# Letting SSD groups two to four wait one product more between asking for the decays' rows and using them

## The chip, the cores and the metric

The kernel runs on one core of a Trainium2 chip. The core has five engines, each with its own queue, which it works off in order: TensorE (PE, matmuls and transposes), VectorE (DVE), ScalarE (ACT), GpSimd (POOL) and SyncE (SP). Data come from HBM by DMA. The metric is the device time of one execution in microseconds; the kernel before took 1976.08 us in the median of three runs (1975.45, 1976.08 and 1978.53).

## The reference

The kernel computes one layer of a decoder trunk for a sequence of 1024 positions of width 1024 in float32. Three token mixers share one input projection; the third is a Mamba-2 SSD, and it is the one that the change touches:

```
h  = h + W_out( sum_k sigmoid(g_k(xn)) * P_k(mixer_k(xn)) ),  xn = RMSNorm(h)
h  = h + W2 relu(W1 RMSNorm(h))^2
...
def ssd_mixer(z, xbc, dt_raw, conv_w, conv_b, dt_bias, a_log, d_skip, norm_g):
    xbc = jax.nn.silu(causal_dwconv(xbc, conv_w, conv_b))
    ...
    a_cs = jnp.cumsum(adt, axis=-1)
    decay = jnp.exp(segsum(adt))
    cb = jnp.einsum('bclgn,bcsgn->bgcls', cc, bc)
    y_diag = jnp.einsum('bgcls,bgrcls,bcsgrp->bclgrp', cb, decay, xdt)
    states = jnp.einsum('bcsgn,bgrcs,bcsgrp->cbgrpn', bc, decay_states, xdt)
    ...
    y_off = jnp.einsum('bclgn,cbgrpn,bgrcl->bclgrp', cc, prev, jnp.exp(a_cs))
    y = y_diag + y_off + x32 * d_skip
```

There are four SSD groups of four heads each, eight chunks of 128 positions, and beside them eight heads of a linear recurrence (RG-LRU) and eight groups of a gated MLP.

## The kernel before, in words

The stretch that matters here is the projection by single columns of 128, run by `run` and `one_unit`. A unit is a product of 128 output channels with all 1024 positions: 48 matmuls of 512 columns (L555), since each operand is split into a high and a low part and three of the four part products are taken. Behind the matmuls `one_unit` calls the unit's `post`, which evicts the product (a convolution for SSD and LRU channels: L576 on ACT, then three L578 on DVE; for a gate L235 to L238), and then `step`, which advances every pending generator to its next `yield`. So a `yield` in a generator is worth one product: what stands behind it is written behind the next product's matmuls. A weight tile of a unit is loaded two units ahead by SP, copied on ACT (L526 for the high part, L527 for the negative of it) and completed by an accumulating DMA on POOL (L528).

The units come in this order for each of the four SSD groups: the channels of B, C, x0 and x1 of the group, then two LRU heads (in the fourth group each head has a gate product behind it), and after all groups the eight gated-MLP products. The first of the two products behind a group's four is called A, the second B.

With x1's eviction a group enters `ssd_stages`. The positions are worked in two halves. `rows_in` asks for the decays' rows of a half: four DMAs on POOL (L657) broadcast rows of `acs_d` to all partitions, into two tiles `E` (named a in the profile). `s1_` asks for the rows' exponentials (L663, POOL), transposes x and B on PE (L669, L676) and multiplies C with B (L681); DVE evicts with L672, L673 and L684, ACT with L677; ACT turns the rows into decays with 16 L690 of 128 columns and two L691; DVE multiplies with L694. `s2_` makes the states (L703 on PE, L714 on DVE), `s3_` the outputs (L723 and L727 on PE, L729 to L731 on DVE) and stores them (L732, POOL). The `aux` tiles in PSUM that PE writes in all these steps come from a pool of four. The LRU heads have stages of their own (L789 on PE, L792 to L801 on ACT, L798 to L804 on DVE, a store L810 on POOL) that use the same pool.

Nothing fixes the order of a queue by hand: the framework orders each engine's instructions from the order in which the program writes them and its own estimate of when each can run. So an instruction may stand earlier in its engine's queue than the program text has it, if its inputs are expected early.

Of the kernel before, what the change touches and what calls it, by code (L numbers as in the profile page):

```python
# [36 lines left out]
def trunk_kernel(ctx: ExitStack, tc: tile.TileContext, x, norm_mix_g, w_in, b_gate, gmlp_ln_g, gmlp_ln_b,  # L37
# [37 lines left out]
    def half_(shape=(P, HF), dt=F32):  # L75
        return halfp.tile(list(shape), dt, tag="half", name=nm("h"))

    def aux():
        return auxp.tile([P, HF], F32, tag="aux", name=nm("aux"))
# [371 lines left out]
    for q in range(2):  # L451
# [3 lines left out]
        for i in range(4):  # L455
            g = q * 4 + i
# [167 lines left out]
    def ssd_units(g):  # L624
        S = {}

        def xbc(key, ct):
            def post(ps):
                c = act()
                conv(c, ps, [scw[:, j * 16 + ct:j * 16 + ct + 1] for j in range(4)], vh[:, SCB + ct:SCB + ct + 1])  # L630
                t = act()
                actv(t, c, AF.Tanh)
                stt(out=c, in0=t, scalar=1.0, in1=c, op0=ALU.add, op1=ALU.mult)
                S[key] = c
                if key == "x1":
                    later(ssd_stages(g, S))
            unit_in(C_XBC + ct * P, post)

        xbc("b", 8 + g)
        xbc("c", 12 + g)  # L640
        xbc("x0", 2 * g)
        xbc("x1", 2 * g + 1)

    def ssd_stages(g, S):
# [5 lines left out]
        def tok(c):  # L650
            return slice(c * P, (c + 1) * P)

        def rows_in(half):
            for q in (2 * half, 2 * half + 1):
                e = E[q] = act((P, 2, 4, P))
                for cc in range(2):
                    nc.gpsimd.dma_start(out=e[:, cc], in_=acs_v[0, 2 * q + cc, hs, :].partition_broadcast(P))  # L657

        def s1_(half):
            for j in range(2):  # L660
                t = er[half, j] = half_((P, 4, P))
                for h in range(2):
                    nc.gpsimd.dma_start(out=t[64 * h:64 * h + 64], in_=acs_v[1, half * 4:half * 4 + 4, 4 * g + 2 * j + h, :].partition_broadcast(64))  # L663
            for q in (2 * half, 2 * half + 1):
                ps = aux()
                for cc in range(2):
                    for j in range(2):
                        o = cc * 256 + j * P
                        nc.tensor.transpose(out=ps[:, o:o + P], in_=Xf[j][:, tok(2 * q + cc)], identity=ident)  # L669
                ev = ps.rearrange("p (c h d) -> p c h d", c=2, h=4)  # L670
                xdt[q], xw[q] = half_((P, 2, 4, 64)), half_((P, 2, 4, 64))
                tt(out=xdt[q], in0=ev, in1=dt[:, 2 * q:2 * q + 2, hs].unsqueeze(3).to_broadcast([P, 2, 4, 64]), op=ALU.mult)  # L672
                tt(out=xw[q], in0=ev, in1=w2[:, 2 * q:2 * q + 2, hs].unsqueeze(3).to_broadcast([P, 2, 4, 64]), op=ALU.mult)  # L673
            ps = aux()
            for i in range(4):
                nc.tensor.transpose(out=ps[:, tok(i)], in_=Bf[:, tok(half * 4 + i)], identity=ident)  # L676
            actv(Bt[:, half * 4:half * 4 + 4, :], ps.rearrange("p (c n) -> p c n", c=4), AF.Copy)  # L677
            cb[half] = aux()
            for i in range(4):
                c = half * 4 + i  # L680
                mm(cb[half][:, tok(i)], Bf[:, tok(c)], Cf[:, tok(c)], start=True, stop=True)  # L681

            cbm = half_((P, 4, P))
            tt(out=cbm, in0=cb[half].rearrange("p (c l) -> p c l", c=4), in1=tri.unsqueeze(1).to_broadcast([P, 4, P]), op=ALU.mult)  # L684
            for q in (2 * half, 2 * half + 1):
                e = E[q]
                for cc in range(2):
                    for h in range(4):
                        col = (2 * q + cc) * 16 + 4 * g + h
                        actv(e[:, cc, h, :], e[:, cc, h, :], AF.Relu, scale=-1.0, bias=acs[:, col:col + 1])  # L690
                actv(e, e, AF.Exp, scale=-1.0)  # L691
                for cc in range(2):
                    i = (2 * q + cc) % 4
                    tt(out=e[:, cc], in0=e[:, cc], in1=cbm[:, i].unsqueeze(1).to_broadcast([P, 4, P]), op=ALU.mult)  # L694
# [38 lines left out]

        rows_in(0)
        yield
        s1_(0)
        yield
        s2_(0)
# [1115 lines left out]
```

## Time and profile before

| | |
|---|---|
| median of the timed runs | 1976.08 us |
| profiled execution, its time | 1979.05 us |
| profiled execution, its span | 1977.3 us |
| mean granted clock of TensorE | 0.986 |
| busy: PE, DVE, ACT, POOL | 1914.5, 1409.4, 1015.5, 256.9 us |

The span is from the first to the last instruction of one profiled execution; its rows are what the sums below are made from. A row's duration is that of the instruction or run of instructions; idle time in square brackets stands before it. Where an instruction waits for several things, the profile names the one that came last.

### The profile page before, as it was taken

Reading aid. Unit: us, or ns where it says so; the run is one execution under the profiler, and the core shown is the slowest. Engines: PE = TensorE matmul, PEld = TensorE weight load, DVE = VectorE, ACT = ScalarE, POOL = GpSimd, SP = SyncE. Lnnn points to the kernel's source line nnn. Section 1 sums busy time; section 2 is a strip of 40 time slices with the busy share of each in tenths; the row PEclk is TensorE's granted clock in tenths of the full one; section 3 lists DMA queues with packets and bytes.
Section 4 is the critical chain, followed back from the end, with each engine's and each line's share of the span. In section 5 each row is a group of like instructions: output and inputs, shape, how many; then the busy total and the mean of one; then the engine's idle time right before and its main releaser. Section 6 shows DMA issues by size and latency. Waiting matters only on the chain.

```text
span 1977.3 us, 23724 instructions
## 1 busy us (share of the span) xinstructions
PE 1914.5 (97%) x8928; PEld 1592.9 (81%) x8928; DVE 1409.4 (71%) x2018; ACT 1015.5 (51%) x1471; POOL 256.9 (13%) x358
## 2 busy tenths in 40 slices
PE   8999999999999999999999999998999999999996
PEld 7998878787887787878778888776788887888885
DVE  5485868686768676767767888347666657788787
ACT  6425858586633545454554544167555555243243
POOL 4111121112233010101010110000211110000000
PEclk8999999999999999999999999999999999999998
DMA  4246574666664252535298987321544458554632
GB/s 158 60 142 138 119 146 112 141 129 138 154 161 128 83 173 87 169 91 165 98 296 277 253 230 191 138 104 60 193 136 165 134 181 303 171 162 117 190 115 88
DMA packets 211015, 301.25 MB, mean 152 GB/s; under 512 B 13028, under 2 KB 125876, under 8 KB 210900
## 3 DMA queue, kind: packets, MB, share of 16 engines
q1 hardware_dynamic: 167348, 158.54, 26.4%
q0 software_dynamic: 34544, 119.69, 22.7%
q10 hardware_dynamic: 9008, 21.51, 3.1%
q8 instruction: 70, 1.15, 0.3%
q14 instruction: 45, 0.37, 0.1%
HBM read 195.75 MB, written 74.58 MB: 137 GB/s over the span
## 4 chain that ended last, share of the span: by engine, by line
PE 68%; DVE 11%; issue 7%; ACT 7%; DMA 6%; POOL 1%; ACTq 0%; POOLq 0%; DVEq 0%; SPq 0%
PE aux L478 39%; PE ps L555 10%; PE gps L478 8%; PE aux L257 5%; PE aux L1376 2%; DMA a<-acs_d 2%; DVE a L578 1%; DMA raw<-in_w_in_dram 1%; DMA c<-yc_d 1%; ACT a L1425 1%; DMA wl<-raw 1%; PE aux L789 1%; DVE a L133 1%; DVE rsq_q L111 1%; DVE wt L133 1%
## 5 line engine op out<-in xcount | busy, mean ns | idle before, releaser
L555 PE MATMUL ps<-xn,wh 128*128 128x512 f32 x1088 | 294.8, 392 | 0.0
L478 PE MATMUL aux<-b,b 128*128 128x512 f32 x1152 | 264.4, 389 | 0.9 <-DVE b L133 0.9
L478 PEld LDWEIGHTS aux<-b,b 128*128 128x128 f32 x1152 | 216.1, 188 | 46.9 <-DVE b L133 1.7
L555 PEld LDWEIGHTS ps<-xn,wh 128*128 128x128 f32 x1088 | 202.9, 188 | 42.1 <-issue 0.7
L478 PE MATMUL aux<-a,b 128*128 128x512 f32 x960 | 219.4, 389 | 0.0
L478 PEld LDWEIGHTS aux<-a,b 128*128 128x128 f32 x960 | 180.2, 188 | 37.4
L555 PE MATMUL ps<-xn,wl 128*128 128x512 f32 x544 | 167.6, 389 | 0.0
L478 PE MATMUL gps<-xn,wt 128*128 128x512 f32 x684 | 160.2, 392 | 2.1 <-DVE a L238 2.1
L478 PE MATMUL aux<-b,wt 128*128 128x512 f32 x672 | 156.9, 389 | 0.0
L478 PEld LDWEIGHTS gps<-xn,wt 128*128 128x128 f32 x684 | 129.4, 189 | 29.4 <-issue 2.5
L478 PEld LDWEIGHTS aux<-b,wt 128*128 128x128 f32 x672 | 126.2, 188 | 26.2
L132 ACT ACTIVATE b<-wt 128x1024 fp32r<-128x1024 f32 x88 | 90.9, 1054 | 85.5 <-DMA wt<-u_d 55.3
L133 DVE TENSOR_TENSOR wt<-a,wt 128x1024 fp32r<-128x1024 f32 x66 | 80.9, 1226 | 66.9 <-ACT wt L132 66.9
L555 PEld LDWEIGHTS ps<-xn,wl 128*128 128x128 f32 x544 | 102.1, 188 | 21.5
L133 DVE TENSOR_TENSOR b<-wt,b 128x1024 fp32r<-128x1024 f32 x88 | 107.2, 1219 | 15.7 <-ACT b L132 15.7
L1606 DVE TENSOR_TENSOR a<-aux,a 128x512 f32<-128x512 f32 x112 | 77.0, 689 | 50.4 <-PE aux L478 50.4
L133 DVE TENSOR_TENSOR a<-a,a 128x1024 fp32r<-128x1024 f32 (+1 forms) x68 | 66.6, 986 | 41.2 <-ACT a L132 41.1
L133 DVE TENSOR_TENSOR wt<-rt,wt 128x1024 fp32r<-128x1024 f32 x35 | 42.9, 1225 | 57.1 <-ACT wt L132 57.0
L478 PE MATMUL aux<-a,wt 128*128 128x512 f32 x336 | 80.3, 396 | 3.3 <-ACT a L1483 3.3
L132 ACT ACTIVATE a<-a 128x1024 fp32r<-128x1024 f32 (+1 forms) x68 | 55.9, 838 | 53.4 <-DVE a L1558 45.1
L478 PEld LDWEIGHTS aux<-a,wt 128*128 128x128 f32 x336 | 64.1, 191 | 17.6 <-ACT a L1483 4.2
L132 ACT ACTIVATE wt<-a 128x1024 fp32r<-128x1024 f32 x66 | 69.6, 1054 | 8.8 <-DVE a L506 8.3
(349 smaller groups left out, 3533.3 us busy)
## 6 DMA issues: line engine op xcount, KB each, us to landing
wt<-u_d SPq DMA_DIRECT2D x54, 512.0 KB
u_d<-a POOLq DMA_DIRECT2D x48, 512.0 KB, 5.4
raw<-in_w_in_dram SPq DMA_DIRECT2D x34, 512.0 KB
wl<-raw POOLq DMA_DIRECT2D x34, 512.0 KB, 5.3
g_d<-a POOLq DMA_DIRECT2D x24, 512.0 KB, 3.4
a<-g_d ACTq DMA_DIRECT2D x24, 512.0 KB
rt<-in_w_in_dram SPq DMA_DIRECT2D x19, 512.0 KB
a<-in_w_in_dram SPq DMA_DIRECT2D x19, 512.0 KB
```

Of the source, the lines that this page charges most:

```text
L111: stt(out=q, in0=r, scalar=nh, in1=r, op0=ALU.mult, op1=ALU.mult)
L132: actv(dst_hi, src, AF.Copy)
L133: (eng or nc.vector).tensor_tensor(out=dst_lo, in0=src, in1=dst_hi.bitcast(F32), op=ALU.subtract)
L257: mm(ps[:, :nt], X.tok(a, k, c), wk[k][w], start=(k == 0 and i == 0), stop=(k == KD - 1 and i == 2))
L478: mm(ps, lhs[l][kk], rhs[r][kk], start=(new and n == 0), stop=(n == 11), skip_group_check=not new)
L555: mm(ps[:, hsl(h)], w[wi][:, k, :], a.rhs(ai, k, h), start=(n == 0), stop=(n == 3 * KD - 1))
L578: stt(out=dst[:, j:], in0=ps[:, :T - j], scalar=taps[3 - j], in1=dst[:, j:], op0=ALU.mult, op1=ALU.add)
L789: mm(ps, w[wi][:, q * P:(q + 1) * P], S["xs"][half][ai], start=(n == 0), stop=(n == 2))
L1376: mm(ps, M.tok(a, k, c), wo[nb][k][w], start=(k == 0 and a + w == 0), stop=(k == KD - 1 and a == 1))
L1425: actv(Nf[th, k // 2][:, k % 2, (c % 4) * P:(c % 4 + 1) * P], ps[:, i * P:(i + 1) * P], AF.Identity, scale=g2c[:, KD + k:KD + k + 1])
L1606: tt(out=h, in0=ps, in1=h, op=ALU.add)
```

## The change

In `ssd_stages`, all groups but the first yield once more between the request for the first half's rows and the first use of them. All later steps of the group, the second half's request among them, come one product later. No instruction is added or taken away.

```diff
         rows_in(0)
         yield
+        if g:
+            yield
         s1_(0)
         yield
         s2_(0)
```

In group one `s1_(0)` still follows product A. In groups two, three and four it followed A and now follows B; `s2_(0)` then follows the next group's first product, and `s3_(1)`, the last step, comes behind A of the next group (before it came behind x1's product, ahead of A).

On PE, around the end of product B in group two, the queue before has the states of `s2_(0)` (L703) and the LRU stage of A's head (L789) between B and the next product; ps is a product, aux a tile of PSUM, h and a tiles in SBUF.

```order
L555 MATMUL ps_2790<-xn_239,wl_2544 128x512
L555 MATMUL ps_2790<-xn_555,wl_2544 128x512
L703 MATMUL aux_2861<-h_2736,a_2641 128x256 x2
L703 MATMUL aux_2873<-h_2745,a_2641 128x256 x2
L789 MATMUL aux_2886<-h_2716,lw_2712 128x512
L789 MATMUL aux_2886<-h_2717,lw_2712 128x512
L789 MATMUL aux_2886<-h_2716,lw_2713 128x512
L789 MATMUL aux_2892<-h_2716,lw_2712 128x512
L789 MATMUL aux_2892<-h_2717,lw_2712 128x512
L789 MATMUL aux_2892<-h_2716,lw_2713 128x512
L555 MATMUL ps_2938<-xn_224,wh_2650 128x512
```

Now the same place reads as follows; L789 has become L791 by the two lines added above it.

```order
L669 MATMUL aux_2815<-ident,a_2597 128x128
L676 MATMUL aux_2824<-ident,a_2239 128x128 x4
L681 MATMUL aux_2830<-a_2391,a_2239 128x128 x4
L791 MATMUL aux_2860<-h_2716,lw_2712 128x512
L791 MATMUL aux_2860<-h_2717,lw_2712 128x512
L791 MATMUL aux_2860<-h_2716,lw_2713 128x512
L555 MATMUL ps_2912<-xn_224,wh_2650 128x512
L555 MATMUL ps_2912<-xn_537,wh_2650 128x512
```

`s1_(0)` stands where `s2_(0)` stood, and three of the LRU stage's matmuls follow directly behind it; the others come later.

On ACT, around A in group three, the queue before has L690 and L691 of the first half's tiles on both sides of L576, which evicts A (ps_3403), and L677 behind it.

```order
L690 ACTIVATE a_3390<-a_3390,acs 128x128 x8
L690 ACTIVATE a_3393<-a_3393,acs 128x128
L691 ACTIVATE a_3390<-a_3390 128x1024
L690 ACTIVATE a_3393<-a_3393,acs 128x128 x6
L576 ACTIVATE a_3452<-ps_3403,va 128x1024
L690 ACTIVATE a_3393<-a_3393,acs 128x128
L677 ACTIVATE a_3389<-aux_3496 128x512
L691 ACTIVATE a_3393<-a_3393 128x1024
L526 ACTIVATE wh_3533<-raw_3531 128x1024
```

Now the eight L690 of the first tile (a_3354) stand ahead of the rows shown here; with the one of the second tile, nine L690, one L691 and an L526 are ahead of A's eviction (ps_3367), and L677 stands behind the eviction of B (ps_3479).

```order
L690 ACTIVATE a_3357<-a_3357,acs 128x128
L691 ACTIVATE a_3354<-a_3354 128x1024
L526 ACTIVATE wh_3474<-raw_3472 128x1024
L576 ACTIVATE a_3416<-ps_3367,va 128x1024
L527 ACTIVATE wl_3475<-wh_3474 128x1024
L690 ACTIVATE a_3357<-a_3357,acs 128x128 x7
L691 ACTIVATE a_3357<-a_3357 128x1024
L132 ACTIVATE h_3428<-a_3416 128x512
L132 ACTIVATE h_3432<-a_3416 128x512
L526 ACTIVATE wh_3655<-raw_3653 128x1024
L576 ACTIVATE a_3528<-ps_3479,va 128x1024
L677 ACTIVATE a_3353<-aux_3572 128x512
```

Six L690 have moved behind A's eviction, and L677 behind B's.

On POOL, the second half's rows of group two (two tiles E, four L657) before:

```order
L732 DMA yr_d<-h_2724 128x512
L732 DMA yr_d<-h_2727 128x512
L657 DMA a_3031<-acs_d 128x512 x2
L657 DMA a_3034<-acs_d 128x512
L810 DMA hr_d<-a_2885 128x1024
L657 DMA a_3034<-acs_d 128x512
L663 DMA h_3147<-acs_d 64x4x128 x2
```

And now, where the program has the second half's request:

```order
L732 DMA yr_d<-h_2803 128x512
L528 DMA wl_3150<-raw_3147 128x1024
L657 DMA a_3141<-acs_d 128x512 x2
L812 DMA hr_d<-a_2995 128x1024
L657 DMA a_3144<-acs_d 128x512 x2
L528 DMA wl_3273<-raw_3270 128x1024
```

Before and now a store of an LRU head (L810, now L812) stands among the four requests; it has two of them behind it now, where it had one.

## Rows read from the trace of the kernel before

**Rows 1.** The page, busy time, share of the span and instructions of each engine.

```profile
PE 1914.5 (97%) x8928; PEld 1592.9 (81%) x8928; DVE 1409.4 (71%) x2018; ACT 1015.5 (51%) x1471; POOL 256.9 (13%) x358
```

**Rows 2.** The table by stage: stretch in us, its length, then for PE, weight loads (PEld), DVE, ACT and POOL the busy time and in brackets the instructions, then the granted clock of TensorE as a share of full speed, DMA share and GB/s.

```profile
280.00:300.00 20.00, 17.38 (x75) 13.63 (x74) 18.26 (x36) 9.88 (x13) 4.67 (x7) 1.00 0.58 106
...
340.00:380.00 40.00, 36.95 (x202) 30.51 (x201) 22.80 (x28) 23.89 (x37) 9.48 (x15) 1.00 0.66 140
...
460.00:480.00 20.00, 16.49 (x64) 12.67 (x63) 14.96 (x27) 14.48 (x23) 7.20 (x11) 0.91 0.66 142
...
540.00:600.00 60.00, 60.00 (x299) 50.84 (x298) 39.19 (x37) 18.12 (x20) 23.34 (x17) 1.00 0.57 150
```

**Rows 3.** The waits from 240 to 500 us: engine, tile and line, what it waited for; us in total, times, longest.

```profile
ACT a L690 <- DMA a<-acs_d: 26.5, 9, 7.8
...
PE aux L703 <- DVE h L673: 4.4, 2, 3.1
...
PE aux L703 <- ACT a L576: 3.0, 1, 3.0
```

**Rows 4.** The timeline of PE in group two: start us, us, engine, line, operation, tiles, shapes, count, and in square brackets the idle time before it with what ended it.

```profile
271.61 1.04 PE L669 MATMUL aux<-ident,a 128*128 128x128 f32 x8
...
273.73 1.17 PE L555 MATMUL ps<-xn,wh 128*128 128x512 f32 x4
...
286.17 2.23 PE L703 MATMUL aux<-h,a 128*128 128x256 f32 x8 [1.29 <-DVE h L673]
...
289.63 1.07 PE L555 MATMUL ps<-xn,wh 128*128 128x512 f32 x4
...
297.91 0.93 PE L789 MATMUL aux<-h,lw 128*128 128x512 f32 x3 [1.32 <-DVE h L714]
```

**Rows 5.** The timeline of ACT in group two; columns as in rows 4.

```profile
271.42 1.28 ACT L690 ACTIVATE a<-a,acs 128x128 f32<-128x128 f32 x4 [7.24 <-DMA a<-acs_d]
...
274.68 0.41 ACT L690 ACTIVATE a<-a,acs 128x128 f32<-128x128 f32 x1 [0.45 <-DMA a<-acs_d]
...
275.94 1.85 ACT L690 ACTIVATE a<-a,acs 128x128 f32<-128x128 f32 x6
277.69 1.19 ACT L576 ACTIVATE a<-ps,va 128x1024 f32<-128x1024 f32 x1
...
279.07 0.58 ACT L677 ACTIVATE a<-aux 128x512 f32<-128x512 f32 x1
...
282.87 1.15 ACT L132 ACTIVATE h<-a 128x512 fp32r<-128x512 f32 x2 [0.22 <-DVE a L578]
284.46 1.06 ACT L526 ACTIVATE wh<-raw 128x1024 fp32r<-128x1024 f32 x1 [0.44 <-PE ps L555]
285.43 1.19 ACT L576 ACTIVATE a<-ps,va 128x1024 f32<-128x1024 f32 x1
```

**Rows 6.** The timeline of DVE in group two; columns as in rows 4.

```profile
278.92 3.92 DVE L578 SCALAR_TENSOR_TENSOR a<-ps,va,a 128x1023 f32<-128x1023 f32 x3 [12.51 <-ACT a L576]
...
286.54 0.68 DVE L673 TENSOR_TENSOR h<-aux,w 128x512 f32<-128x512 f32 x1
```

**Rows 7.** The timeline of PE in groups three and four; columns as in rows 4.

```profile
362.35 1.03 PE L669 MATMUL aux<-ident,a 128*128 128x128 f32 x8
...
378.67 2.79 PE L703 MATMUL aux<-h,a 128*128 128x256 f32 x8 [3.04 <-ACT a L576]
...
383.73 1.09 PE L555 MATMUL ps<-xn,wh 128*128 128x512 f32 x4
...
454.93 1.03 PE L669 MATMUL aux<-ident,a 128*128 128x128 f32 x8
...
471.32 3.18 PE L703 MATMUL aux<-h,a 128*128 128x256 f32 x8 [3.11 <-DVE h L673]
...
476.37 1.09 PE L555 MATMUL ps<-xn,wh 128*128 128x512 f32 x4
...
478.31 0.93 PE L789 MATMUL aux<-h,lw 128*128 128x512 f32 x3 [0.40 <-ACT a L237]
```

**Rows 8.** The timeline of ACT in groups three and four, the eviction of the group's first LRU product; columns as in rows 4.

```profile
370.19 1.19 ACT L576 ACTIVATE a<-ps,va 128x1024 f32<-128x1024 f32 x1
...
462.84 1.20 ACT L576 ACTIVATE a<-ps,va 128x1024 f32<-128x1024 f32 x1
```

**Rows 9.** The timeline of POOL, the request for the rows of group two's first half; and from the DMA issues of the whole program all such requests: tiles, issuing engine, operation, count, KB of one, median us from issue to landing.

```profile
264.10 2.49 POOL L657 DMA_DIRECT2D a<-acs_d  x4
...
a<-acs_d POOLq DMA_DIRECT2D x32, 256.0 KB, 7.0
```

**Rows 10.** The chain of waits in order of time, a product that runs undisturbed: start us, us, what.

```profile
129.00 10.91 PE ps L555 x48
```

**Rows 11.** The timeline of PE at the switch from the projection to the stage behind it; columns as in rows 4.

```profile
616.75 2.98 PE L478 MATMUL gps<-xn,wt 128*128 128x512 f32 x12
621.83 4.57 PE L478 MATMUL gps<-xn,wt 128*128 128x512 f32 x12 [2.10 <-DVE a L238]
```

**Rows 12.** The timeline of PE at s3_(1) of group one: its first row, and the product behind it; columns as in rows 4.

```profile
256.47 1.05 PE L723 MATMUL aux<-a,h 128*128 128x128 f32 x8
...
260.59 1.19 PE L555 MATMUL ps<-xn,wh 128*128 128x512 f32 x4
```

## The prediction

> **What bounds the kernel now.** I read the page first: PE is busy 97% of the span [rows 1], so a change in this kernel is worth what it takes from, or adds to, PE's idle time and PE's clock. The table by stage, read next, shows where PE idles while the SSD groups run: 20 − 17.38 = 2.62 us in 280 to 300, 40 − 36.95 = 3.05 in 340 to 380, 20 − 16.49 = 3.51 in 460 to 480 [rows 2], 9.18 in all, one place for each of the three groups that the change touches. The waits name the place: L703, the state products of step s2_, stands still for DVE's L673 or ACT's L576 [rows 3].
>
> The timelines then show why. Call A and B the two products behind a group's four SSD products (LRU heads; in group four B is a gate). In group two A ends at 271.61 and s1_(0) follows at once on PE [rows 4]. ACT has been standing at the first L690 since the group's rows were asked for, 7.24 us, and gets the third tile's piece only at 274.68; L576, which evicts A, is queued behind and starts at 277.69 [rows 5], 6.1 us after A's end. DVE has been idle 12.51 us when it gets A's convolution at 278.92, and has L672 and L673 last at 286.54 [rows 6]. B ended, and PE waited 1.29 us for L673, later 1.32 for L714 [rows 4]. In groups three and four L576 starts 370.19 − 362.35 = 7.8 and 462.84 − 454.93 = 7.9 us after A's end, and PE waits 3.04 and 3.11 us, in group four 0.40 more [rows 7, 8].
>
> A wait of 3 us costs more than itself. L703 and L789 behind it take 383.73 − 378.67 = 5.06 and 476.37 − 471.32 = 5.05 us [rows 7], against 289.63 − 286.17 = 3.46 for the same instructions after the 1.29 us wait [rows 4]: 1.6 us each. So the three places hold 2.61, 3.04 + 1.6 = 4.64 and 3.51 + 1.6 = 5.11 us, 12.4 together.
>
> **The change part by part.** Nothing is added or removed on any engine; s1_(0) and all behind it in groups two to four come one product later. The rows are asked for by the same L657, four DMAs from 264.10 in group two, and a rows DMA takes 7.0 us to land in the median [rows 9].
>
> 1. *The wait of ACT for the rows.* The listing of ACT for group three shows that the L690 are not moved behind A's eviction: nine L690 and one L691 still stand before L576, 15 and one before the change. ACT will therefore still stand for the rows. I price this at nothing gained by itself; it counts through the time at which L576 runs, which I leave at 6 to 8 us after A's end. What changes is who needs it, and when.
>
> 2. *Group two.* Group one isn't moved, so nothing is put between A and B, and B follows A directly: it ends at 271.61 + 10.9 [rows 10] = 282.5. s1_ on PE takes 273.73 − 271.61 = 2.12 [rows 4], to 284.6. Right behind it now stands an L789 of A's head, which needs an aux buffer; s1_ has taken all four, and the one that it is given is freed by ACT's L677. On ACT, L677 stands behind B's eviction. From the rows: A's L576 at 277.69 − 2 x 0.31 (two L690 fewer) + 1.05 (an L526 now ahead) = 278.1; A's convolution 0.4 later than before, done at 283.3; two L132 to 284.4; L526, B's L576 and L677 by their spacing in [rows 5] to 287.1. PE waits 287.1 − 284.6 = 2.5 us. Bounds: 1.3 if ACT is a row earlier, 3.1 as in group four. One wait of 2.5 replaces two of 1.3. Whether it also slows PE's clock is bounded by two rows: 1.3 didn't [rows 4], a wait of 2.10 at the stage switch did, twelve matmuls of 512 columns taking 4.57 instead of 2.98 [rows 11]. The nearer row is the second, so I take 1.6. A later L789 waits for a buffer that an L792 frees, behind table loads on ACT: 0.4 by the row of its kind in [rows 7]. Group two: 2.5 + 1.6 + 0.4 = 4.5 against 2.61, **+1.9** (−0.9 to +2.5).
>
> 3. *Group three.* Here group two's s3_(1), also a product later now, lands between A and B: 260.59 − 256.47 = 4.1 us of PE [rows 12]. From A's end, B ends at 4.1 + 10.9 = 15.0 and L789 is reached at 17.1. A's L576 at 6.1 to 7.9 is followed 1.2 later by 3.9 of convolution, with two steps of s3_(1) in it of L673's shape (0.7 each [rows 6]), to 12.6 to 14.4, and by two L132 of 1.1 to 13.7 to 15.5: the old stall is covered by s3_(1) and B but for half a us. What is late next is L677, behind L526 and L576 of B, which wait for B's end: 15.0 or 15.5 + 1.0 + 1.1 + 0.6, 17.7 to 18.2, a wait of 0.6 to 1.1; I take 0.8. The later L789 adds 0.5. 1.3 against 4.64, **−3.3** (0 to −4.6).
>
> 4. *Group four.* The same cover; the first L789 needs DVE's L673, behind the same convolution (12.6 to 14.4), two more steps of s3_(1), two L133 and an L672 of 0.6 to 0.7 each: 16.3 to 18.1 against 17.1, so 0.6, and the following three share ACT with the gate's L235 and L237: 0.7. 1.3 against 5.11, **−3.8** (−1 to −5.1).
>
> 5. *The second half's rows.* rows_in(1) moves along too, and on POOL two of its four L657 come to stand behind a store of an LRU head, which waits for that head's scan. Issued about when s1_(1) begins, they make ACT stand up to 7 us more at L690, ahead of L632 and the next eviction. s1_(1) has two products until s3_(1) needs its result, so I cost it at 0.5 (0 to 3 per group).
>
> 6. *Behind 500 us.* PE has no idle time from 540 to 600 and DVE is busy 39.19 of 60 [rows 2]: the late steps of group four fit there, at nothing. What PE gains arrives at the end, since no other engine comes near its 97%.
>
> Sum: +1.9 − 3.3 − 3.8 + 0.5 = −4.7 us. Against the profiled execution's 1979.05 that is 1974.35; the median of the timed runs is 2.97 lower, and 1976.08 − 4.7 = **1971.4**.
>
> The Trainium skill (TensorE: Matmul & The Clock Gate, "HAM oscillation — how this bites in real kernels") says that each wait that lets the clock fall pays for the climb again. By it one wait in group two is dearer than two short ones, which the two rows on either side bear out; without that price the sum would be −6.3.
>
> **The rivals.** *Renamed wait.* ACT runs its queue in order, and the L690 that wait for rows are still ahead of L576. If A's eviction comes later than 8 us after A's end in groups three and four too, or if L677 there slips behind other work, L789 waits as in group two: 4.5 in each of three groups, 13.5 against 12.4, **1977.2**. For it: ACT's 26.5 us at L690 in nine waits [rows 3] and the unchanged POOL queue. Against: in groups three and four 4.1 us stand between A and B that don't in group two. The Trainium skill (the same page, "Architectural detail: the array is 16× 32×32, not 1× 128×128") calls ACT and DVE strict FIFO; by that rule an earlier request helps nobody whose instruction is queued behind the waiter, and the 7.24 us row agrees.
>
> *Everything hidden.* If L677 and L673 run in time in all three groups, all 12.4 go: **1963.7**. For it: DVE's 12.51 us of idle time before A's convolution [rows 6], room to be earlier. Against: four aux buffers, filled by s1_.
>
> *The second half's rows are late* (the slower side). The L657 behind the LRU store land 7 us after it; ACT, blocked, delays the eviction of x0's and x1's products and with it L714. From the point at which that delay passes some 2 us, PE waits at L723 in each group, 2 us and 1.6 of clock: 3 x 3.6 = 10.8 on top of the forecast's −4.7, **1982.2**. For it: the order of POOL; against: two products of slack.
>
> **How the numbers follow.** Less than 0.2%, 3.95 us, is what a measurement of this kernel can't tell from no change. Forecast 0.45, renamed wait 0.27, everything hidden 0.13, late rows 0.15. The forecast's own range is 1968.5 to 1975; two thirds of its chance I put below 1972.1. So faster is 0.30 + 0.13 + 0.05 (a cheap case of the renamed wait) = 0.48; same is 0.15 + 0.18 = 0.33; slower, the late rows and the dear end of the renamed wait, 0.19. For 8 in 10 the range takes in all but the far half of the hidden case and of the late rows: 1965.5 to 1980.
>
> **What would show it.** Right: PE's waits at L703 are gone in all three groups; an L789 waits for ACT's L677 by about 2.5 us in group two and under 1 in group three; ACT's waits at L690 remain, some 7 us each; one clock drop instead of two, near 285. Wrong: waits of 2.5 or more at L789 in groups three and four (renamed), PE idle at L723 (late rows), or PE without idle time in group two (hidden).

## The result, and the profile after

The changed kernel takes 1965.37 us in the median of four runs (1964.1 to 1968.92), beside 1975.99 us for the kernel before (four runs, 1975.45 to 1978.53): a ratio of 0.9948 [0.9936, 0.996], 10.6 us less. The prediction was 1971.4 us with a range of 1965.5 to 1980.0: the direction and the mechanism hold, but the gain is more than twice the 4.7 us of the sum, right at the range's lower end (0.1 us under it in the medians; by the ratio 0.9948 x 1976.08 = 1965.8, just above it) and nearest to the rival that hides everything (1963.7).

The page after, busy time of each engine. PE lost 9 us of busy time though it does the same matmuls [rows 1]; they run at full pace more often (mean granted clock 0.991, 0.986 before). Some 5 of the 9 us lie in the stretch of the SSD groups, which is taken apart below.

```profile
PE 1905.5 (97%) x8928; PEld 1587.2 (81%) x8928; DVE 1407.0 (72%) x2018; ACT 1014.6 (52%) x1471; POOL 262.5 (13%) x358
```

The table by stage after, the stretches of [rows 2]. PE's idle time is 20 − 18.27 = 1.73 us in the first (2.62 before), 0.07 in the second (3.05) and none in the third (3.51); from 540 to 600 it has none, as before. The granted clock, 0.91 from 460 to 480 before, is 1.00.

```profile
280.00:300.00 20.00, 18.27 (x90) 15.37 (x89) 15.86 (x27) 13.24 (x19) 3.72 (x6) 1.00 0.59 117
...
340.00:380.00 40.00, 39.93 (x217) 33.37 (x216) 26.36 (x42) 22.04 (x37) 9.38 (x14) 1.00 0.66 144
...
460.00:480.00 20.00, 20.00 (x91) 16.56 (x89) 18.03 (x23) 14.26 (x21) 2.88 (x5) 1.00 0.61 151
...
540.00:600.00 60.00, 60.00 (x308) 51.22 (x308) 37.25 (x38) 20.41 (x24) 27.88 (x16) 1.00 0.50 139
```

The waits after, from 240 to 545 us. PE's waits at L703 [rows 3] are gone, and one of 1.7 us at L791 is left. ACT still stands 22.9 us at L690 (27.0 before in the same stretch). So the change left most of the standing where it was and took most of those who suffered from it out of its way.

```profile
ACT a L690 <- DMA a<-acs_d: 22.9, 10, 7.0
...
PE aux L791 <- ACT a L677: 1.7, 1, 1.7
```

The timeline of PE after, in groups two, three and four; it answers to [rows 4, 7]. A ends at 268.70 in group two, at 353.62 in group three, and B at 279.58 and 368.75.

```profile
279.58 1.04 PE L669 MATMUL aux<-ident,a 128*128 128x128 f32 x8
...
280.89 1.06 PE L681 MATMUL aux<-a,a 128*128 128x128 f32 x8
283.67 0.96 PE L791 MATMUL aux<-h,lw 128*128 128x512 f32 x3 [1.73 <-ACT a L677]
284.47 1.09 PE L555 MATMUL ps<-xn,wh 128*128 128x512 f32 x4
...
297.41 1.89 PE L703 MATMUL aux<-h,a 128*128 128x256 f32 x8
298.95 1.72 PE L791 MATMUL aux<-h,lw 128*128 128x512 f32 x6
300.51 0.62 PE L555 MATMUL ps<-xn,wh 128*128 128x512 f32 x2
...
353.62 1.05 PE L723 MATMUL aux<-a,h 128*128 128x128 f32 x8
...
357.74 1.19 PE L555 MATMUL ps<-xn,wh 128*128 128x512 f32 x4
...
368.75 1.04 PE L669 MATMUL aux<-ident,a 128*128 128x128 f32 x8
...
371.19 0.98 PE L791 MATMUL aux<-h,lw 128*128 128x512 f32 x3
...
458.43 0.93 PE L791 MATMUL aux<-h,lw 128*128 128x512 f32 x3
```

The reader sees s3_(1) (L723) between A and B in group three, and L791 behind s1_ with no bracket there and in group four. The block of eight L703 and six L791, which nothing holds up now, takes 300.51 − 297.41 = 3.10 us. Before, the same instructions took 3.46 behind a wait of 1.29 us, and 5.06 and 5.05 behind those of 3.04 and 3.11. The step from 3.10 to 3.46 is one more wait for DVE, inside the block: in all three groups the weight load of the fifth L703 stood 0.40 us for the second of the two L673 (in group two it ended at 286.54 + 0.68 = 287.22 [rows 6], and the load follows at 287.27). The step from 3.46 to 5.06 is the clock, which fell there to the lower of its two levels, 1.2 GHz (mean granted 0.78 of full speed from 378 to 382 us and 0.67 from 471 to 475).

The timeline of ACT after, in groups two and three; it answers to [rows 5, 8].

```profile
268.26 1.28 ACT L690 ACTIVATE a<-a,acs 128x128 f32<-128x128 f32 x4 [6.99 <-DMA a<-acs_d]
...
274.77 1.19 ACT L576 ACTIVATE a<-ps,va 128x1024 f32<-128x1024 f32 x1
...
281.00 1.04 ACT L526 ACTIVATE wh<-raw 128x1024 fp32r<-128x1024 f32 x1
281.95 1.19 ACT L576 ACTIVATE a<-ps,va 128x1024 f32<-128x1024 f32 x1
283.04 0.58 ACT L677 ACTIVATE a<-aux 128x512 f32<-128x512 f32 x1
...
352.68 2.64 ACT L690 ACTIVATE a<-a,acs 128x128 f32<-128x128 f32 x8 [3.89 <-DMA a<-acs_d]
...
357.99 1.19 ACT L576 ACTIVATE a<-ps,va 128x1024 f32<-128x1024 f32 x1
...
368.50 1.06 ACT L526 ACTIVATE wh<-raw 128x1024 fp32r<-128x1024 f32 x1 [3.17 <-PE ps L555]
369.46 1.19 ACT L576 ACTIVATE a<-ps,va 128x1024 f32<-128x1024 f32 x1
370.55 0.59 ACT L677 ACTIVATE a<-aux 128x512 f32<-128x512 f32 x1
```

Where the time came from is read between two products. x1's product of group two starts at 245.39 us before and 242.48 after, the twentieth product behind it at 551.56 and 536.06: 306.17 against 293.58, so 12.6 us are saved there. PE's waits in that stretch fell from 9.16 (the two of group two, 3.04, 3.11 and 0.40) to 1.73, 7.4 less; the three L703 blocks from 3.46 + 5.06 + 5.05 = 13.57 to 3 x 3.10 = 9.30, 4.3 less, of which 3 x 0.36 = 1.1 is the wait for the second L673 and 2 x 1.6 = 3.2 the clock. The other 0.9 us is spread over single matmuls and wasn't taken apart. Of the 14.9 us between the two spans another 3.0 were there before the first product (it starts at 128.84 and 125.84), which isn't the change's, and 0.6 is given back behind the stretch. The timed medians put the change at 10.6.

### The profile page after: what moved, and what is told of

Read it like the earlier page. It is cut to its first block, busy times and chain, and to the rows that moved or that the text cites. A ratio compares the mean times of both kernels' runs of the same rounds, so it can differ in the third digit from the quotient of the medians.

```text
span 1962.4 us, 23743 instructions
## 1 busy us (share of the span) xinstructions
PE 1905.5 (97%) x8928; PEld 1587.2 (81%) x8928; DVE 1407.0 (72%) x2018; ACT 1014.6 (52%) x1471; POOL 262.5 (13%) x358
## 4 chain that ended last, share of the span: by engine, by line
PE 82%; DVE 8%; ACT 5%; DMA 3%; issue 2%; POOL 0%; ACTq 0%; SPq 0%; DVEq 0%; POOLq 0%
PE aux L478 40%; PE ps L555 18%; PE gps L478 11%; PE aux L257 4%; PE aux L1378 2%; PE aux L791 1%; DMA c<-yc_d 1%; PE aux L727 1%; PE aux L723 1%; ACT a L1427 1%; PE aux L703 1%; DVE a L133 1%; DVE rsq_q L111 1%; ACT wt L132 1%; DMA a<-g_d 1%
## 5 line engine op out<-in xcount | busy, mean ns | idle before, releaser
L133 DVE TENSOR_TENSOR b<-wt,b 128x1024 fp32r<-128x1024 f32 x88 | 107.2, 1219 | 15.5 <-ACT b L132 15.5
```

Source lines behind the costliest of these rows:

```text
L133: (eng or nc.vector).tensor_tensor(out=dst_lo, in0=src, in1=dst_hi.bitcast(F32), op=ALU.subtract)
```

## The experiments

The theory under test: ACT, held at L690 by the rows' DMAs, evicts A late, and the change helps because s3_(1) and B stand between A and the first step that needs it. The rivals: that the time comes from one group, that an earlier request alone would do, or that the extra product itself is needed. Each kernel has the kernel before beside it on the same chip: 1975.37 us for one group, two groups and the earlier request; 1977.15 for all groups, the order kept and the rows on SP; 1974.84, on another chip, for the last four.

### One group alone, and two

Only group two:

```diff
-        if g:
+        if g == 1:
             yield
```

> Only group two yields once more. Theory (cover): the time comes from what PE finds between product A and the first step that needs DVE or ACT, above all the preceding group's s3_(1), 4.1 us, which lands between A and B of the next group once its own group is moved. Then group two changes as in the changed kernel (its two waits of 1.3 us become one of about 1.7 at L791 for L677), and group three, though not moved itself, loses its 3.0 us wait at L703 and its clock drop, because group two's s3_(1) now stands between its A and B; group four keeps its 3.1 us. In time 1.2 + 5.2, about -6.4 us, 1969.6. Rival (rows): the time comes from the product more that a moved group's rows have to land, each group for itself; then group three keeps its 3.0 us wait and only group two gains, -1 to -3 us, 1973 to 1975.

Measured 1973.14 us, 0.9987 [0.9979, 0.9996]. The waits of PE in this kernel from 240 to 545 us, the timeline of PE in group three, and the table of two stretches there:

```profile
PE aux L703 <- DVE h L673: 2.6, 1, 2.6
PE aux L791 <- ACT a L677: 2.4, 1, 2.4
PE aux L669 <- DVE h L730: 1.8, 1, 1.8
```

```profile
360.82 0.81 PE L669 MATMUL aux<-ident,a 128*128 128x128 f32 x4 [1.79 <-DVE h L730]
361.29 2.06 PE L555 MATMUL ps<-xn,wh 128*128 128x512 f32 x4
```

```profile
359.00:363.00 4.00, 2.21 (x9) 1.90 (x9) 4.00 (x5) 4.00 (x9) 0.09 (x1) 0.77 0.00 0
363.00:367.00 4.00, 4.00 (x17) 3.21 (x17) 3.90 (x7) 2.06 (x4) 2.63 (x4) 0.80 0.71 163
```

The time is the one that the rival named (1973 to 1975), not the theory's 1969.6; the trace shows why, and not for the rival's reason. Group two's two waits became one of 2.36 (forecast 1.7), and no clock fell behind it. In group three the wait at L703 went and another came: s3_(1) of group two and s1_(0) of group three now follow A together, with no B between them, and L669 waits for an aux buffer until DVE's L730, queued behind A's late convolution, frees it. The matmuls behind it run for a while at the lower level of the clock (mean granted 0.77 and 0.80 in the two stretches), and most of the gain is lost. A group that moves alone pushes its last step onto the next group's first.

Groups three and four:

```diff
-        if g:
+        if g > 1:
             yield
```

> Only groups three and four yield once more. Cover: group two is as before (1.29 and 1.32 us); group three is moved but has no s3_(1) between its A and B, so it looks as group two does in the changed kernel, one wait of 1.5 to 2.5 us at L791 for ACT's L677; group four has no wait. About -3 and -5.7, -8.7 us, 1967.3. Rows: groups three and four both without any wait, -5.2 and -5.7, -10.9 us, 1965.

Measured 1972.11 us, 0.9974 [0.9962, 0.9985], less gain than theory and rival gave (1967.3 and 1965). Group two has 0.94 and 1.30 (1.29 and 1.32 before), group four has none, and group three, which is now the first to move and has no s3_(1) between A and B, has what group two has in the changed kernel, only longer (PE's timeline):

```profile
376.74 0.96 PE L791 MATMUL aux<-h,lw 128*128 128x512 f32 x3 [4.06 <-ACT a L677]
377.54 1.83 PE L555 MATMUL ps<-xn,wh 128*128 128x512 f32 x4
```

Only group four:

```diff
-        if g:
+        if g == 3:
             yield
```

> Only group four yields once more. Cover: groups two and three as before; group four has no s3_(1) between A and B, so a wait of 1.5 to 2.5 us stays at its first L791 or L703 in place of 3.1 and 0.4 us and the clock drop: about -3.5 us, 1972.5. Rows: group four without any wait, -5.7 us, 1970.3.

Measured 1974.31 us, 0.9992 [0.9984, 1.0001], so no gain that can be told from none, where 1972.5 and 1970.3 were forecast. Group four, first to move here, has one wait for two (PE's timeline):

```profile
468.10 0.93 PE L791 MATMUL aux<-h,lw 128*128 128x512 f32 x3 [3.14 <-DVE h L673]
468.87 1.07 PE L555 MATMUL ps<-xn,wh 128*128 128x512 f32 x4
```

The three runs agree on one thing: the first group that moves is left with one wait at L791 (2.36, 4.06, 3.14; in group four it is for L673 and not for L677). A moved group behind another moved one, group four in the second run and groups three and four in the changed kernel, has no such wait, because s3_(1) of the group before stands between A and B. The wait stays with whoever is first. In time all three runs gained less than the theory forecast, which didn't see the new wait in group three or the length of the one that stays.

All four groups:

```diff
-        if g:
-            yield
+        yield
```

> All four groups yield once more. Cover: group one has no PE wait to lose, but its s3_(1) now stands between A and B of group two, which so gets the cover that it lacked; the 1.7 us at L791 there go, and group one, like group two in the changed kernel, may get one wait of up to 2 us at its own L791: 1963 to 1966. Rival (rows): nothing changes in groups two to four, group one gains or loses under 1 us by itself, 1965 with the 1.7 us wait still in group two.

Measured 1964.89 us, 0.9936 [0.9923, 0.9948]. Group two now has group one's s3_(1) between its A and B, and PE waits nowhere from 240 to 545 us, though ACT still stands 21.2 us at L690. The theory had forecast 1963 to 1966 without group two's wait of 1.73 us. That wait is about 0.1% of the run, and the intervals of the two kernels overlap.

### Without the extra product: the cause itself

In the kernel before, the first half's L690 of groups two to four are kept at their place in the program's order (a hint to the framework, which the kernel before also gives, for the loads of the LRU weights and one ACT instruction, but nowhere in these stages), so that none can float ahead of A's eviction; no yield is added:

```diff
-                        actv(e[:, cc, h, :], e[:, cc, h, :], AF.Relu, scale=-1.0, bias=acs[:, col:col + 1])
+                        i_ = actv(e[:, cc, h, :], e[:, cc, h, :], AF.Relu, scale=-1.0, bias=acs[:, col:col + 1])
+                        if half == 0 and g:
+                            tc.keep_in_program_order(i_)
```

> The kernel before with nothing moved but the L690 of the first halves of groups two to four, which are pinned behind what the program writes ahead of them on ACT; so A's L576 stands ahead of all 16 and needs no rows. Theory (ACT standing for the rows in front of an eviction is the cause, and the change only covers it): A's L576 starts within about 1.5 us of A's end, L673 is through before B ends, the waits at L703 and L789 (2.6, 3.0, 3.5 us) and both clock drops go: about -11 us, 1964, as fast as the changed kernel without moving a step. Rival (the place of the steps): the five evictions of s1_(0) and the convolutions of A and B don't fit between A and L703 whatever ACT does; a wait of 1 us or more stays at L703 in each group and less than half is gained, 1970 or above.

Measured 1962.57 us, 0.9924 [0.991, 0.9938]. The timeline of ACT in group two, and two stretches of the table:

```profile
269.41 1.06 ACT L526 ACTIVATE wh<-raw 128x1024 fp32r<-128x1024 f32 x1 [7.17 <-PE ps L555]
270.38 1.19 ACT L576 ACTIVATE a<-ps,va 128x1024 f32<-128x1024 f32 x1
271.46 0.59 ACT L677 ACTIVATE a<-aux 128x512 f32<-128x512 f32 x1
271.94 2.44 ACT L690 ACTIVATE a<-a,acs 128x128 f32<-128x128 f32 x8
```

```profile
280.00:300.00 20.00, 20.00 (x105) 16.77 (x104) 15.74 (x34) 11.25 (x16) 1.25 (x2) 1.00 0.55 105
...
340.00:380.00 40.00, 40.00 (x218) 33.63 (x217) 28.09 (x43) 23.07 (x38) 8.76 (x14) 1.00 0.79 168
```

ACT idles before A as long as before (7.17 us), but for PE, not for the rows. L576 comes first, L690 behind it finds its rows landed, and PE has no wait. With nothing moved by a product, all that the change gained is there, and the rival that the steps don't fit is out. The hint takes L677 ahead of the L690 along with L576; the run with the rows on SP, below, leaves both behind the L690.

The same, on the changed kernel:

> The changed kernel with the L690 of the same halves pinned in the same way. Theory: the one wait left, 1.7 us at L791 in group two, goes too, since A's and B's L576 are in time there: 0.5 to 2 us faster than the changed kernel, 1963 to 1965. Rival (the wait is the price of four aux buffers taken by s1_, not of the late eviction): L677 still comes too late for L791, a wait of 1 us or more stays, time as the changed kernel, 1965.4, or above where the later L690 make L694 late.

Measured 1964.69 us, 0.9938 [0.9925, 0.995], no wait of PE. It adds nothing that can be told from the changed kernel, which has only the 1.73 us left to give.

In the kernel before, the rows are asked for on SP instead of POOL:

```diff
-                    nc.gpsimd.dma_start(out=e[:, cc], in_=acs_v[0, 2 * q + cc, hs, :].partition_broadcast(P))
+                    nc.sync.dma_start(out=e[:, cc], in_=acs_v[0, 2 * q + cc, hs, :].partition_broadcast(P))
```

> The kernel before with the rows asked for on SP's queue instead of POOL's, every other step where it was. Theory: what counts is how long ACT stands at the first L690s. If the rows land sooner after A's convolution needs ACT (their issue on SP isn't behind a weight's accumulating DMA, or their landing is shorter than the 7 to 10 us of before), PE's waits shrink by as much as A's L576 comes earlier, up to -11 us; if they land as late, the time stays within 3 us of before and ACT's waits at L690 are 7 us as before.

Measured 1964.17 us, 0.9939 [0.9927, 0.9951]; PE waits nowhere from 240 to 545 us. From its waits and ACT's timeline:

```profile
ACT a L690 <- DMA a<-acs_d: 2.5, 4, 0.9
```

```profile
261.95 2.44 ACT L690 ACTIVATE a<-a,acs 128x128 f32<-128x128 f32 x8
...
269.67 1.21 ACT L576 ACTIVATE a<-ps,va 128x1024 f32<-128x1024 f32 x1 [1.69 <-PE ps L555]
```

Here 15 L690 still stand ahead of A's eviction, and that does no harm, because their rows are there: ACT stands 2.5 us for them (27.0 in ten waits in this stretch before), and A's L576 waits for PE alone. Order and lateness are both needed to make the stall; taking away either one ends it. One reason that the rows are there is that they are asked for earlier: in group two SP issues the four L657 13.7 us after the start of x1's product (256.95 − 243.25), POOL did so after 18.7 (264.10 [rows 9] − 245.39). On POOL they stood behind an L528 that itself waited for ACT (POOL before, then SP in this run):

```profile
263.00 0.86 POOL L528 DMA_DIRECT2D wl<-raw  x1 [8.95 <-ACT wl L527]
```

```profile
256.95 1.96 SPq L657 DMA_DIRECT2D a<-acs_d  x4
```

### Asking earlier

In the kernel before, the stages of groups two to four are started one product earlier, so that the request comes a product earlier and all else where it was:

```diff
-                if key == "x1":
+                if key == ("x0" if g else "x1"):
                     later(ssd_stages(g, S))
...
         yield
+        if g:
+            yield
         s1_(0)
```

> The kernel before, with the rows of groups two to four asked for one product earlier (behind x0's product) and every other step where it was. If ACT's standing at L690 in front of A's eviction is what makes DVE late (part of the theory, and of the rows rival too), the waits at L703 and L789 in all three groups go without moving a step, and the two clock drops with them: about -12 us, 1964. If instead the place of s1_ and s2_ themselves is what matters (too little time between A and L703 for the convolution and the five evictions), the waits stay above 1.5 us and the time within 4 us of before.

Measured 1981.6 us, 1.0027 [1.0017, 1.0038], slower. From its waits, and the timeline of ACT in group two (line numbers are two lower in the stages, so L667, L688 and L689 are L669, L690 and L691):

```profile
PE aux L667 <- DVE a L633: 11.6, 3, 4.7
```

```profile
265.12 1.06 ACT L526 ACTIVATE wh<-raw 128x1024 fp32r<-128x1024 f32 x1 [9.22 <-DMA raw<-in_w_in_dram]
...
267.34 2.73 ACT L688 ACTIVATE a<-a,acs 128x128 f32<-128x128 f32 x9
269.97 1.04 ACT L689 ACTIVATE a<-a 128x1024 f32<-128x1024 f32 x1
270.92 1.04 ACT L632 ACTIVATE a<-a 128x1024 f32<-128x1024 f32 x1
```

The L690 moved forward with the request. They no longer wait for rows, but nine of them and an L691 now stand before L632, the SiLU of x1, for 270.92 − 267.34 = 3.6 us; PE's transposes of x1 need it at once, and wait 3.37, 3.50 and 4.71 us. The waits at L703 are gone, as forecast, and dearer ones have come, which were not. ACT's other wait there, 9.22 us for a weight tile, could be to blame as well; so the L690 were kept in program order in this kernel:

> The kernel of the early request (rows asked for one product earlier, every other step where it was before), with the L690 pinned as in the pinned kernel. Theory (the early request lost because the L690 came forward with it and stood in front of the eviction of x1's product): the waits at the first transposes, 3.4 to 4.7 us per group, go, and the time is that of the pinned kernel, 0.991 to 0.994 of before. Rival (the early request itself is harmful: its tiles or its transfers collide with others): it stays at or above before, 1.000 or more.

Measured 1963.16 us, 0.994 [0.9927, 0.9953]. ACT waits as long for the weight tiles (26.4 us in three waits, 27.7 without the hint), and PE has 0.4 us of waits left at the transposes:

```profile
ACT wh L526 <- DMA raw<-in_w_in_dram: 26.4, 3, 9.8
...
PE aux L667 <- DVE a L633: 0.4, 1, 0.4
```

So the weight tile cost next to nothing, and it was the place of the L690 that cost; the rival that the early request harms by itself is out.

### Is there more to gain?

Three runs on the chip of the last kernel: the changed kernel again, the L690 of both halves kept in order (without the yield), and the first half's kept in order with the rows on SP.

> The changed kernel once more, beside the next three on one chip: 0.994 to 0.995 of before, one PE wait in group two, between 1 and 3 us by when the rows land in that execution.

> The kernel before with the L690 of both halves of groups two to four pinned. Theory: the second halves have two products of slack, so pinning them changes nothing beyond the pinned kernel, 0.991 to 0.994; a wait of PE at L723 would show that they had less.

> The pinned kernel with the rows asked for on SP as well. Theory: nothing is left to gain between the tenth and the thirtieth product, each of the two alone leaves no PE wait there; the same time as either within 2 us, 0.991 to 0.994. If the waits for the rows still cost anything behind the pinned L690, this one is faster by more than 2 us.

Measured 1963.65 us, 0.9944 [0.9932, 0.9956]; 1963.68, 0.994 [0.9928, 0.9952]; 1963.28, 0.994 [0.9928, 0.9952]. With 1963.16 for the kernel above, four kernels lie within 0.5 us. In the two others PE has no wait in the stretch; the changed kernel repeats its one, of 1.8 us. All ways out of the stall end at 0.992 to 0.994 of the kernel before, where PE has nothing left to wait for in the stretch, and the change comes within one wait of it. Whether the kernel with the order kept and no yield (0.9924) beats the changed one isn't settled: the two weren't timed side by side, and its nearest relatives here show no difference.

## Why the prediction was right or wrong

**What bounds the kernel** held: each us that came off PE's waits and clock came off the span, and the place was the one named.

**The mechanism** held in its parts: L703's waits are gone, the wait that is left in group two is at L791 for L677, and ACT still stands for the rows. The runs show the cause, too: L690 kept behind A's eviction, or rows that come early, give the same gain. "Some 7 us each" for those waits held in group two (6.99), not in groups three and four (3.89 and 3.10). "One clock drop, near 285" didn't come; from 240 to 545 us there is none.

**The sizes** failed, 12.6 us in the profiles where the sum had 4.7. By waits and blocks, with the same blocks compared:

| | forecast | measured | how |
|---|---|---|---|
| group two | +1.9 | −1.2 | waits 2.61 to 1.73, block 3.46 to 3.10 |
| group three | −3.3 | −5.0 | wait 3.04 to 0, block 5.06 to 3.10 |
| group four | −3.8 | −5.5 | waits 3.51 to 0, block 5.05 to 3.10 |
| second half's rows | +0.5 | 0 | no wait of PE at L723 |

*Group two* is the largest miss, 3.1 us, and half of it is the clock. The wait of 2.5 measured 1.73: L677 ended 14.9 us after A's end (283.62 − 268.70; forecast 15.5), 0.6 early. Another 0.24 is bookkeeping: the profile counts idle time from the end of s1_'s last matmul, 2.36 us after its first began, and the prediction counted from the 2.12 at which the next product followed; the matmuls are as fast as before. The 1.6 us for a fall of the clock never came: the product behind the wait starts at 284.47 at full pace. I had bounded it by a wait of 1.29 without a fall and one of 2.10 with one, and took the nearer row; the last section shows that the length of a wait doesn't decide this by itself. The Trainium skill (TensorE: Matmul & The Clock Gate, "HAM oscillation — how this bites in real kernels") was weighed for the same term, that each wait which lets the clock fall pays for the climb; this wait let nothing fall. The 0.4 for a later buffer was absent as well.

*Group three.* The step "what is late next is L677" was right, and the wait was mis-sized: some 0.3 us where 0.8 was taken. From A's end L677 was done at 17.5 us (371.14 − 353.62; forecast 17.7 to 18.2), and L791 started at once, at 17.6, where 17.1 was forecast. In group four, where nothing holds it, L791 follows 2.12 us after s1_ begins (458.43 − 456.31), here after 2.44, so it stood for L677; the trace has its weight load idle 0.3 us for L677, and PE itself the 0.07 us of the table. A's L576 came 4.4 us after A's end, not 6.1 to 7.9, as ACT stood 3.89 us and not 7. The 0.5 for a later buffer was absent.

*Group four* had the same two terms, 0.6 and 0.7, and neither came: from A's end DVE ended the L673 that L791 needs at 17.1 us, and PE got there at 17.3. Here and in group three, a few tenths of a us at each end of an estimate were the whole term.

*The block behind a wait.* I took 3.46 us, the block behind the 1.29 us wait, for the undisturbed one. Undisturbed it is 3.10, and the 0.36 is the wait for the second L673, which the prediction left out in all three groups. The 1.6 us for a fall of the clock, 5.06 − 3.46, stands. So what the three places held was 9.16 of waits and 13.57 − 9.30 = 4.27 behind them, 13.4 us and not 12.4. That adds 0.36 in each group.

**The rivals.** *Everything hidden* was nearly the case, with 1.73 us left. *Renamed wait* is what happens to the first group that moves, and the 4.06 and 3.14 us of the runs in which groups three and four move first show it there; it was wrong here for the reason that was given against it, the s3_(1) between A and B. *Late rows* didn't happen. What the prediction didn't see is how the groups depend on each other: it priced them one by one. In the profiles the stretch from x1's product of group two to the twentieth behind it takes 303.15 us in the run of group two alone (242.47 to 545.62) and 300.76 in that of groups three and four (242.81 to 543.57), 3.0 and 5.4 less than before, together 8.4 and not the 12.6 of all three. The ratios say the same (2.6 and 5.1 us, 7.7 and not 10.3), though their intervals are too wide to prove it alone; the new wait at L669 in group three shows where the rest goes.

The Trainium skill calls ACT a strict FIFO (TensorE: Matmul & The Clock Gate, "Architectural detail: the array is 16× 32×32, not 1× 128×128"), and the traces agree: in the slower run L632 stands behind 3.6 us of L690 and L691. What the prediction drew from it, that an earlier request helps nobody who is queued behind the waiter, doesn't hold as it stands. With the rows on SP the request is 5 us earlier, L576 is queued behind L690 as before, and it is helped; in the slower run the request came so early that the L690 moved, too.

## What to carry to other kernels

Where an engine stands for a transfer, look at what is queued behind it and who needs that first: the stall went away equally well by moving the need a product later, by keeping the waiting instructions behind the urgent one, and by bringing the data earlier. But asking a whole product earlier, with nothing else done, made it worse, because the framework moved the consumers forward too. A shift of one stage in a chain of groups is judged as a whole, since each group's last step is the next one's cover. And when estimated terms of half a us decide between a wait and none, count the case of none as likely as the wait.

## What the hardware showed that was not expected

The clock of TensorE doesn't fall by the length of the last wait alone. Waits of 1.73 us (the changed kernel), 1.94 and 3.14 (the run of group four alone, in groups three and four) and 2.36 (the run of group two alone) were followed by a granted clock of 1.00 and matmuls at full pace. Those of 1.79 (the run of group two alone, above), 2.10 (before [rows 11], granted clock 0.66 from 621 to 626 us), 3.04 and 3.11 (before, in groups three and four) and 4.06 (the run of groups three and four) were followed by a fall. At the switch of stage the changed kernel has the same wait as before and this time nothing falls (1.00 from 606 to 610), and the next one, of 2.36, does it (0.62 from 612 to 616; PE's timeline of the changed kernel):

```profile
606.35 3.00 PE L478 MATMUL gps<-xn,wt 128*128 128x512 f32 x12 [2.09 <-DVE a L238]
...
612.25 4.06 PE L478 MATMUL aux<-h,wt 128*128 128x512 f32 x10 [2.36 <-DVE wt L133]
```

Twelve matmuls take 3.00 us behind the first, ten take 4.06 behind the second. What tells the cases apart stays open; a fall is a risk to be given a chance, not a price for each wait over a bound.

The rows' DMAs come in time when SP issues them: 2.5 us of standing instead of 27.0, with the same transfers. Most of that is the earlier request, 5.0 us in group two. The rest is a shorter time to land: the first L690 ran 5.0 us after the first request without waiting (261.95 − 256.95), where on POOL it ran after 7.3 and had waited (271.42 − 264.10). Whether the queue itself or the moment of the request makes the landing shorter wasn't separated.
